# Two projections get the low halves of their weights from ScalarE and an accumulating DMA instead of VectorE

## The chip, the cores and the metric

One core of a Trainium2 chip runs the whole layer, in one launch. The metric is the device time of that launch in microseconds (us); lower is better. Three runs of the kernel before gave 801.69, 801.78 and 803.82 us, so the median is 801.78 us.

The engines that matter here are PE (TensorE, matrix products), ACT (ScalarE), DVE (VectorE), POOL (GpSimd) and SP, which issues most DMAs. Each engine works through its own list of instructions strictly in order. A DMA that an engine issues runs on 16 DMA engines afterwards; the issuing engine waits only until the DMA may start.

## The reference, cut to what matters

The input is 512 tokens of width 1024 in float32. One normalised copy `h` of it is multiplied by one wide weight, and the result is cut into the inputs of two branches (an mLSTM and a sparse attention) and of two gates:

```python
h = rmsnorm(x, norm1_w)
proj = h @ w_in
(mq, mk, mv, mo, mi, mf, nq, kc, vc, ks, vs, kw, vw, ng, gm, gn) = jnp.split(proj, split_pts, axis=-1)
...
kc_t = to_groups(apply_rope(rmsnorm(kv_heads(kc), kcmp_norm_w), cos, sin))
kw_t = to_groups(apply_rope(rmsnorm(kv_heads(kw), kwin_norm_w), cos, sin))
...
x = x + y @ w_out
return x + (a * v) @ ffn_w_down
```

`kw` and `vw` are the third keys and values (of the window attention), `ng` its gates, `mi` and `mf` the mLSTM's gates, `mv` the mLSTM's values.

## The kernel before

All products that are large run as three matmuls over split operands. A float32 weight is split into a high half H (rounded to the type fp32r that PE takes at its fast rate) and a low half L, which is the weight less H. The activations are split the same way, into `hTH` and `hTL`. The product is then the sum of activation-high by H, activation-high by L, and activation-low by H (`mm3`, lines 424 to 427). In the profile these three matmuls have the lines 425, 426 and 427, so line 426 is the first that needs L.

**How a weight comes in.** The class `Weights` (from line 31) handles this for every weight. A chunk of up to 1 MB is loaded by a DMA of SP into one of two `raw` buffers (line 68). A chunk has two halves (in the count of this text: C0 and C1 are the halves of the first chunk of projection C). `ensure` (from line 71) converts half after half into one of four `whl` buffers, which hold H and L side by side. H is always a copy on ACT (line 88). L has three forms, chosen by sets that are filled at lines 291 to 294:

- DVE subtracts (line 94), the form for the halves of the change in the kernel before;
- POOL subtracts (line 94 as well, two halves at the start);
- ACT writes the rounded negative of the weight (line 91), and POOL issues a DMA that adds the raw weight to it (line 92).

`ensure` also issues the load of the next chunk (line 68) once the chunk two before it has been used. That load overwrites the `raw` buffer of that earlier chunk, so SP holds it until whatever reads this buffer last is done: the subtractions of DVE, or the accumulating DMAs.

**The order of the work.** The order on every engine is written out by hand through a table of numbers (`PLAN`, from line 104). Projection B (first keys and values, 512 columns) runs first. The next projections form one stream, `proj_stream` (from line 743): C (288 columns: `kw`, `vw`, `ng`, `mi`, `mf`), A (queries, 512 columns), MV (the mLSTM's values, 512 columns), then gates and others. A `Filler` hands out this stream step by step between the steps of the attention's preparation. `tok_group` (line 456) calls `ensure` for the half three ahead, at a step that the table names. So A0 is converted at the end of C's second quarter; C0 to C2 are converted during the last token tile of B (line 651), and C3 in C's first quarter.

The preparation of attention follows in the program after the conversions of A0. It begins with `rope_norm` (line 658): squares on ACT (line 667), sums on DVE (line 668), then the rope of the first keys on DVE. Behind that rope, still in DVE's order, stand the copies of the gate columns out of the accumulators of C (`evac_c`, line 703, done by line 235). The accumulators of A's first two token tiles lie in the two PSUM buffers that C's first two tiles used, so PE can begin A only when these copies are done. The compression of the keys and values (line 785, `ph`) needs the sums that DVE writes at line 778.

The lines that the change and the steps of the prediction touch are these: 68 (load of raw), 88 and 91 (ACT), 92 (DMA of POOL), 94 (DVE), 235 (copies), 425 to 427 (matmuls of C, A and MV), 667 and 668 (`rope_norm`), 778 and 785 (compression), 683 (part of the rope on POOL), 846 to 849 (transposes of the queries).

Of the kernel before, what the change touches and what calls it, by code (L numbers as in the profile page):

```python
# [97 lines left out]
def bcast(ap, n):  # L98
# [18 lines left out]
    "p_sc21": 0, "p_sc30": 0, "p_sc31": 1, "poolA": 2, "poolC": 0, "poolGM": 2, "poolGN": 2, "poolMO": 2,  # L117
    "poolMQK": 2, "poolMV": 0, "poolUM": 2, "poolUN": 2, "poolWO": 2, "q2_eb": 1, "q2_ex0": 0, "q2_ex1": 0,
# [1520 lines left out]
```

## Time and profile before

| what | value |
|---|---|
| median of three runs | 801.78 us |
| the profiled execution's own time | 804.88 us |
| span of its instructions | 803.0 us |
| share of the span in which PE works on matmuls | 97% |
| DVE, ACT, POOL busy | 57%, 47%, 27% |
| bytes moved by DMA, mean rate | 132.18 MB, 165 GB/s |
| mean granted clock of PE | 0.993 of full speed |

The profiled execution is 3.1 us (0.4%) longer than the median of the plain runs. The span runs from the first instruction to the last one. Start times in the rows below are microseconds from the span's start. Lines of a timeline give the start, the duration, the engine, the line of the kernel, the operation, what it writes and reads, its shape, how many were merged, and in brackets the idle time of this engine just before and what ended it.

### The profile page before, as it was taken

The page shows a single profiled execution, that of the slowest core. Times are in us where ns is not written, and L with a number is a line of the kernel's source. Part 1 is how long each engine was busy: PE and PEld are TensorE (multiplying, and loading weights), DVE is VectorE, ACT ScalarE, POOL GpSimd, SP SyncE. Part 2 cuts the span into 40 slices and gives each one's busy share as a digit, 9 for nine tenths or more (in the row PEclk, how much of TensorE's full clock was granted, in tenths as well). Part 3 has the DMA queues.
Part 4 walks back from the last instruction along what each step waited for, and adds up shares of the span by engine and source line. Part 5 has one row for each costly group of instructions (what it writes and reads, how often), then busy time and mean ns, then how long its engine had stood idle before and what let it go on. Part 6 is the DMA issues. An engine that isn't in the chain of part 4 may idle for free.

```text
span 803.0 us, 10557 instructions
## 1 busy us (share of the span) xinstructions
PE 779.3 (97%) x4037; PEld 643.3 (80%) x4037; DVE 460.2 (57%) x817; ACT 379.5 (47%) x637; POOL 218.9 (27%) x227
## 2 busy tenths in 40 slices
PE   8999989999999999999879999999999999999898
PEld 5797878878788878878668998888888888888786
DVE  4576775686565654544525545554554554554776
ACT  6344546645565595583523343333333333443552
POOL 5320121220111122122200008855554443200600
PEclk9999999999999999999999999999999999999999
DMA  6884168565555567359885338675545444575372
GB/s 229 279 225 141 20 140 131 106 113 98 105 105 106 106 105 131 79 114 184 183 284 190 147 108 293 239 251 210 199 174 194 178 145 158 204 274 177 120 232 107
DMA packets 97059, 132.18 MB, mean 165 GB/s; under 512 B 6607, under 2 KB 75375, under 8 KB 95600
## 3 DMA queue, kind: packets, MB, share of 16 engines
q1 hardware_dynamic: 63054, 91.64, 34.4%
q0 software_dynamic: 33952, 39.85, 24.4%
q8 instruction: 32, 0.52, 0.3%
q14 instruction: 19, 0.16, 0.1%
q10 hardware_dynamic: 2, 0.00, 0.0%
HBM read 94.79 MB, written 15.73 MB: 138 GB/s over the span
## 4 chain that ended last, share of the span: by engine, by line
PE 73%; issue 8%; DMA 7%; DVE 6%; ACT 4%; POOL 2%; POOLq 0%; SPq 0%; DVEq 0%; ACTq 0%
PE ff L1355 10%; PE ff L1354 10%; PE ff L1356 10%; DMA whl<-raw 4%; PE P L426 3%; PE P L427 3%; PE P L425 2%; PE on L946 2%; PE ptp L935 2%; PE gm L487 1%; PE gm L489 1%; PE gm L488 1%; PE sp L905 1%; PE wo L426 1%; PE wo L427 1%
## 5 line engine op out<-in xcount | busy, mean ns | idle before, releaser
L88 ACT ACTIVATE whl<-raw 128x1024 fp32r<-128x1024 f32 (+2 forms) x144 | 144.9, 1011 | 145.0 <-PE ff L1356 57.2
L94 DVE TENSOR_TENSOR whl<-raw,whl 128x1024 fp32r<-128x1024 f32 (+1 forms) x102 | 127.6, 1260 | 146.0 <-ACT whl L88 146.0
L1354 PE MATMUL ff<-h2H,whl 128*128 128x512 f32 (+1 forms) x384 | 142.8, 372 | 0.0
L1355 PE MATMUL ff<-h2L,whl 128*128 128x512 f32 (+1 forms) x384 | 142.6, 371 | 0.0
L1356 PE MATMUL ff<-h2H,whl 128*128 128x512 f32 (+1 forms) x384 | 142.6, 371 | 0.0
L92 POOL DMA_DIRECT2D whl<-raw x40 | 54.8, 1371 | 231.6 <-ACT whl L91 223.0
L1354 PEld LDWEIGHTS ff<-h2H,whl 128*128 128x128 f32 x384 | 72.3, 188 | 12.6
L1356 PEld LDWEIGHTS ff<-h2H,whl 128*128 128x128 f32 x384 | 72.3, 188 | 12.5
L1355 PEld LDWEIGHTS ff<-h2L,whl 128*128 128x128 f32 x384 | 72.3, 188 | 12.3
L920 ACT ACTIVATE P<-sp,nmx 128x128 f32<-128x128 f32 (+3 forms) x64 | 33.1, 524 | 36.7 <-DVE nmx L911 36.5
L91 ACT ACTIVATE whl<-raw 128x1024 fp32r<-128x1024 f32 x40 | 41.9, 1048 | 0.0
L1406 ACT ACTIVATE ct<-ct 128x512 f32<-128x512 f32 x22 | 13.9, 633 | 54.1 <-DVE ct L1404 54.1
L911 DVE TENSOR_REDUCE nmx<-sp 128x2 f32<-128x256 f32 (+3 forms) x32 | 26.2, 818 | 17.9 <-PE sp L908 17.8
L425 PE MATMUL P<-whl,g 128*128 128x512 f32 x88 | 34.2, 389 | 0.0
L426 PE MATMUL P<-whl,g 128*128 128x512 f32 x88 | 34.2, 389 | 0.0
L427 PE MATMUL P<-whl,g 128*128 128x512 f32 x88 | 34.2, 389 | 0.0
L1404 DVE SCALAR_TENSOR_TENSOR ct<-ff,vcol,ct 128x511 f32<-128x511 f32 (+1 forms) x44 | 32.7, 744 | 2.2 <-ACT ct L1402 1.4
L1412 ACT ACTIVATE g<-ct 128x512 fp32r<-128x512 f32 x22 | 13.9, 632 | 37.0 <-DVE ct L1416 21.9
L426 PE MATMUL wo<-whl,yH 128*128 128x512 f32 x64 | 25.6, 400 | 4.1 <-DMA whl<-raw 4.1
L235 DVE COPY P<-ptp 128x256 f32<-128x256 f32 (+1 forms) x32 | 17.7, 554 | 19.3 <-PE ptp L935 19.2
L426 PE MATMUL P<-whl,sb 128*128 128x512 f32 x66 | 25.9, 393 | 2.5 <-DVE whl L94 2.3
L1413 DVE TENSOR_TENSOR g<-ct,g 128x512 fp32r<-128x512 f32 x22 | 15.4, 699 | 21.9 <-ACT g L1412 21.9
(400 smaller groups left out, 1795.0 us busy)
## 6 DMA issues: line engine op xcount, KB each, us to landing
raw<-in_ffn_w_up_dram SPq DMA_DIRECT2D x22, 1024.0 KB, 5.1
whl<-raw POOLq DMA_DIRECT2D x40, 512.0 KB, 5.7
raw<-in_w_in_dram SPq DMA_DIRECT2D x16, 1024.0 KB, 5.0
st<-in_ffn_w_down_dram SPq DMA_DIRECT2D x11, 1024.0 KB, 7.5
td<-st POOLq DMA_DIRECT2D x11, 1024.0 KB, 4.2
raw<-td SPq DMA_DIRECT2D x22, 512.0 KB, 5.4
raw<-in_ffn_w_down_dram SPq DMA_DIRECT2D x11, 512.0 KB, 4.2
raw<-in_w_out_dram SPq DMA_DIRECT2D x4, 1024.0 KB, 8.1
```

Source lines behind the costliest of these rows:

```text
L88: nc.scalar.activation(h, src, AF.Copy)
L91: nc.scalar.activation(l, src, AF.Copy, scale=-1.0)
L92: nc.gpsimd.dma_start(l, src, accum_op=ALU.add)
L94: (nc.gpsimd if n in self.on_pool else nc.vector).tensor_sub(l, src, h)
L425: pe.matmul(o, aH, bH, start=start, stop=False)
L426: pe.matmul(o, aH, bL, start=False, stop=False)
L427: pe.matmul(o, aL, bH, start=False, stop=stop)
L920: act.activation(Pv[:, y], sv[:, y], AF.Exp, bias=nmx[:, y:y + 1], accum_out=den[:, y:y + 1])
L1354: pe.matmul(acc[:, a:b], H[:, k, :], hh, start=(k == 0), stop=False)
L1355: pe.matmul(acc[:, a:b], H[:, k, :], hl, start=False, stop=False)
L1356: pe.matmul(acc[:, a:b], L[:, k, :], hh, start=False, stop=(k == KD - 1))
L1404: dve.scalar_tensor_tensor(t[:, k:], a[:, :S - k], col("ffn_conv_w", (2 - k) * NF + m), t[:, k:], op0=ALU.mult, op1=ALU.add)
```

## The change

Two numbers of the table become 2. With 2, all halves of a projection go into the set `on_dma`, and their low half takes the third of the forms above. With 0, none of them do. The projections are C (`poolC`) and MV (`poolMV`), each with four halves. A half of C has 2 x 288 = 576 columns of float32 in each of 128 partitions (294,912 bytes), a half of MV 2 x 512 = 1024 (524,288 bytes). Nothing else is changed: neither the places at which the halves are converted nor the order of the other work.

```diff
-    "p_sc21": 0, "p_sc30": 0, "p_sc31": 1, "poolA": 2, "poolC": 0, "poolGM": 2, "poolGN": 2, "poolMO": 2,
-    "poolMQK": 2, "poolMV": 0, "poolUM": 2, "poolUN": 2, "poolWO": 2, "q2_eb": 1, "q2_ex0": 0, "q2_ex1": 0,
+    "p_sc21": 0, "p_sc30": 0, "p_sc31": 1, "poolA": 2, "poolC": 2, "poolGM": 2, "poolGN": 2, "poolMO": 2,
+    "poolMQK": 2, "poolMV": 2, "poolUM": 2, "poolUN": 2, "poolWO": 2, "q2_eb": 1, "q2_ex0": 0, "q2_ex1": 0,
```

The lines of `ensure` between which the sets choose are these:

```python
nc.scalar.activation(h, src, AF.Copy)
if n in self.on_dma:

    nc.scalar.activation(l, src, AF.Copy, scale=-1.0)
    nc.gpsimd.dma_start(l, src, accum_op=ALU.add)
else:
    (nc.gpsimd if n in self.on_pool else nc.vector).tensor_sub(l, src, h)
```

## Rows read from the trace of the kernel before

**Rows 1.** Busy time of each engine in three stretches (from and to, length, then PE, PEld, DVE, ACT and POOL with busy us and instructions, PE's granted clock, share and rate of the DMA engines). The first holds projection C and the start of A, the second the rest of A, the third MV.

```profile
30.00:60.00 30.00, 29.82 (x179) 26.47 (x177) 19.24 (x44) 13.20 (x25) 4.26 (x5) 1.00 0.84 242
60.00:94.00 34.00, 33.65 (x204) 27.16 (x203) 23.52 (x52) 16.64 (x30) 1.61 (x4) 1.00 0.30 87
94.00:118.00 24.00, 21.62 (x113) 17.43 (x112) 20.43 (x32) 8.98 (x14) 6.90 (x6) 1.00 0.59 120
```

**Rows 2.** What PE waited for between 30 and 130 us, longest first (total us, times, longest).

```profile
PE pq L846 <- DVE qdup L235: 1.8, 3, 1.1
PE pq L846 <- ACT qdup L233: 0.6, 1, 0.6
```

**Rows 3.** The group of DVE's subtractions for low halves between 30 and 130 us (count, then busy us and mean ns, then idle time before).

```profile
L94 DVE TENSOR_TENSOR whl<-raw,whl 128x576 fp32r<-128x576 f32 (+1 forms) x8 | 7.9, 988 | 6.3 <-ACT whl L88 6.3
```

**Rows 4.** ACT's timeline from the conversion of C0 to the squares of `rope_norm`. The four conversions with 576 columns are C0 to C3; those at 43.76 and 44.72 are H and the negative of A0.

```profile
35.29 0.69 ACT L88 ACTIVATE whl<-raw 128x576 fp32r<-128x576 f32 x1 [3.88 <-issue]
37.11 0.69 ACT L88 ACTIVATE whl<-raw 128x576 fp32r<-128x576 f32 x1 [1.13 <-PE aBs L427]
39.22 0.69 ACT L88 ACTIVATE whl<-raw 128x576 fp32r<-128x576 f32 x1 [1.42 <-DMA raw<-in_w_in_dram]
...
40.07 0.67 ACT L88 ACTIVATE whl<-raw 128x576 fp32r<-128x576 f32 x1
43.76 1.06 ACT L88 ACTIVATE whl<-raw 128x1024 fp32r<-128x1024 f32 x1 [3.01 <-DMA raw<-in_w_in_dram]
44.72 1.04 ACT L91 ACTIVATE whl<-raw 128x1024 fp32r<-128x1024 f32 x1
45.67 0.61 ACT L667 ACTIVATE rqk<-kraw 128x512 f32<-128x512 f32 x1
```

**Rows 5.** SP's timeline, three of its loads of raw chunks: the first chunk of A at 38.62, the first of MV at 55.08, and the second of the gates (GM) at 98.42.

```profile
38.62 0.37 SPq L68 DMA_DIRECT2D raw<-in_w_in_dram  x1
...
55.08 0.37 SPq L68 DMA_DIRECT2D raw<-in_w_in_dram  x1
...
98.42 0.37 SPq L68 DMA_DIRECT2D raw<-in_w_in_dram  x1
```

**Rows 6.** POOL's timeline: its DMAs for A0 and A1, then a part of the first query's rope and the DMA of GM0.

```profile
46.08 1.07 POOL L92 DMA_DIRECT2D whl<-raw  x1 [17.92 <-ACT whl L91]
50.51 0.87 POOL L92 DMA_DIRECT2D whl<-raw  x1 [3.35 <-ACT whl L91]
...
94.50 0.88 POOL L683 TENSOR_TENSOR rtq<-qraw,tab 128x256 f32<-128x256 f32 x1 [26.08 <-DVE qraw L679]
96.05 1.61 POOL L92 DMA_DIRECT2D whl<-raw  x1 [0.67 <-ACT whl L91]
```

**Rows 7.** All accumulating DMAs up to 130 us from issue to landing; a DMA of POOL of 256 KB (count, KB, median us to landing); and the busy times (columns as in the first group) of the two microseconds in which the DMA of A0 moved its 512 KB.

```profile
DMA to landing us min/median/max: 4.4/5.6/6.1
...
out_dram<-x1r POOLq DMA_DIRECT2D x2, 256.0 KB, 2.5
...
48.00:50.00 2.00, 2.00 (x17) 2.00 (x16) 1.43 (x6) 1.97 (x4) 0.00 (x0) 1.00 1.12 217
```

**Rows 8.** DVE's timeline: the subtraction for C1, the sums of `rope_norm`, the copies of the gate columns of C's first two token tiles, the sums for the compression, and the subtraction for MV3 with what follows it.

```profile
37.83 0.76 DVE L94 TENSOR_TENSOR whl<-raw,whl 128x576 fp32r<-128x576 f32 x1 [0.96 <-ACT whl L88]
...
46.32 1.28 DVE L668 TENSOR_REDUCE rss<-rqk 128x8 f32<-128x512 f32 x2 [3.56 <-ACT rqk L667]
...
52.44 0.28 DVE L235 COPY gts<-aC 128x32 f32<-128x32 f32 x2
...
61.63 2.67 DVE L778 TENSOR_TENSOR X<-pz,pet 64x496 f32<-64x496 f32 x4
...
97.18 1.21 DVE L94 TENSOR_TENSOR whl<-raw,whl 128x1024 fp32r<-128x1024 f32 x1
98.70 1.30 DVE L849 TENSOR_TENSOR QS<-pq,QS 64x512 fp32r<-64x512 f32 x2 [0.32 <-ACT QS L848]
```

**Rows 9.** PE's timeline: the first matmul of C that needs a low half, and the first matmul of A; then from the chain of waits the start of the compression (start, length).

```profile
39.70 0.29 PE L426 MATMUL aC<-whl,hTH 128*128 128x288 f32 x1
...
53.12 0.47 PE L425 MATMUL aA<-whl,hTH 128*128 128x512 f32 x1
...
64.55 7.13 PE ph L785 x64
```

**Rows 10.** ACT's timeline, two places: the copies of H of MV3 and GM0 (merged), and that of GM2, the first half of GM's second chunk.

```profile
92.60 2.20 ACT L88 ACTIVATE whl<-raw 128x1024 fp32r<-128x1024 f32 x2
...
117.26 1.04 ACT L88 ACTIVATE whl<-raw 128x1024 fp32r<-128x1024 f32 x1
```

**Rows 11.** Busy times (columns as in the first group) in three pairs of stretches: one in which PE stood idle for most of the time, and one soon after it.

```profile
10.00:12.00 2.00, 0.18 (x2) 0.07 (x1) 0.09 (x1) 1.76 (x4) 2.00 (x2) 1.00 1.05 309
13.00:17.00 4.00, 4.00 (x14) 3.08 (x13) 3.36 (x9) 2.30 (x4) 1.84 (x3) 0.57 0.69 264
...
384.00:387.00 3.00, 0.43 (x2) 0.00 (x0) 0.69 (x2) 2.28 (x3) 0.88 (x1) 1.00 0.55 88
389.00:392.00 3.00, 3.00 (x8) 2.30 (x7) 2.25 (x4) 2.51 (x3) 0.82 (x1) 0.50 1.03 304
...
414.00:418.00 4.00, 0.31 (x2) 0.00 (x0) 0.00 (x0) 0.48 (x1) 0.00 (x0) 1.00 0.72 205
419.50:422.50 3.00, 3.00 (x8) 2.31 (x7) 1.47 (x2) 0.03 (x1) 0.00 (x0) 0.50 0.96 310
```

## The prediction

> **What bounds the kernel now.** I read the busy times by stretch first, then PE's waits, then the timelines of ACT, SP, POOL, DVE and PE around projection C. In the first two stretches PE is busy for 29.82 of 30 us and 33.65 of 34 us [rows 1], so PE sets the pace there and DVE, with 19.24 and 23.52 us, does not. In the third, PE is idle for 2.38 us, and its waits for the queries' rope account for it, 1.8 + 0.6 us [rows 2]. So work taken from DVE can only win in that third stretch, and anything that makes PE late earlier goes straight into the time.
>
> What to see in ACT's timeline is that the supply of weights is tight at one place. ACT stood idle for 3.01 us until the raw chunk of A had landed, converted A0 at 43.76, wrote its negative at 44.72, and only then could start the squares of `rope_norm` at 45.67 [rows 4]. DVE waited 3.56 us for these squares [rows 8]. So the landing of A's first chunk sets the start of a chain on ACT and DVE. SP issued that load at 38.62 [rows 5], right when DVE's subtraction for C1 ended, 37.83 + 0.76 = 38.59 [rows 8]: C0 and C1 lie in the `raw` buffer that the load overwrites.
>
> **The change part by part.** Removed are eight subtractions, 7.9 us of DVE [rows 3]. Added are eight activations on ACT and eight DMAs on POOL.
>
> *C0 and C1, on the path.* Copies of 576 columns that follow each other would start 0.59 us apart (a copy of 1024 columns takes 1.06 us and its successor starts after 0.96 us, so 0.10 us less than the 0.69 us of one [rows 4]). So C1's H starts at 37.11, its negative at 37.70, ending near 38.38. POOL's DMA for A0 started 0.32 us after its negative ended (44.72 + 1.04 = 45.76 to 46.08 [rows 4, 6]); C1's would start at 38.70.
>
> How long until the sum has landed? The nearest row is A1's DMA of 512 KB: issued at 50.51, and SP, which waits for it, goes on at 55.08, so 4.57 us [rows 5, 6]. Such a DMA moves 217 GB/s [rows 7], so 0.524 MB takes 2.42 us, and C's 0.295 MB 1.36 us: I take 4.57 - 1.06 = 3.5 us. The ends of the range are 2.5 us (a POOL DMA of 256 KB without a sum) and 6.1 us (the slowest accumulating one up to 130 us) [rows 7]. So C1 is done at 42.2 and SP issues A's load 3.6 us later than before. C2's and C3's own accumulating DMAs then run beside that load; alone each moves for 1.36 us, and I take 0.5 us of delay from them (ends 0 and 1.4). A's chunk lands 4.1 us late; call this S.
>
> A rule speaks for a smaller S. The Trainium skill, page "DMA: Bandwidth & Descriptors", section "Anatomy of one DMA — SWDGE (gpsimd) path", puts one such DMA at some 2.0 us plus its bytes at 436 GB/s. That is an estimate of 2.68 us for C1 and an S of 3.2 us. For A1's 512 KB it gives 3.20 us where the trace has 4.57 us, so I stay with the row.
>
> ACT is idle before A0 [rows 4], so S shifts A0's conversion, the squares, and DVE's chain behind them in full. In that chain stand the copies of C's gate columns at 52.44 [rows 8]; two merged in 0.28 us, so the first is out by 52.62. A's first matmul started at 53.12 [rows 9] and needs the accumulator that the copy frees: 0.50 us of margin, so PE begins A 4.1 - 0.5 = 3.6 us late.
>
> *The low half of C0, inside that.* By the same steps C0's negative ends at 36.56, its DMA starts at 36.88 and lands at 40.4, or at 41.4 by the full 4.57 us; PE wants it at 39.70 [rows 9]. PE stands for 0.7 to 1.7 us. This does not add to the 3.6 us, because PE would only wait less before A: some 1.9 to 2.9 us.
>
> *PE's clock.* In three places PE stood idle: 1.82 of 2 us from 10, most of 384 to 387, and 3.69 of 4 us from 414. Soon after each the granted clock was 0.57 or 0.50, the lower of its two levels (1.2 GHz) for most or all of the stretch. Eight matmuls took 3.00 us from 389 to 392 and from 419.5 to 422.5 [rows 11]; at the full clock they take half, so each drop costs 1.5 us, and 1.6 us with its edges. The waits before the queries' transposes, none over 1.1 us [rows 2], left the clock at 1.00 [rows 1]. A wait of 1.9 to 2.9 us lies on the side of those that lost the clock. I take a drop as somewhat likelier than none: 3.6 + 1.6 = 5.2 us.
>
> Without a drop another margin sets the sum: DVE's sums for the compression end at 64.30 [rows 8] and the compression started at 64.55 [rows 9], 0.25 us later. They follow S, so PE is 4.1 - 0.25 = 3.85 us late there.
>
> *C2, C3, MV0 to MV3, beside other work.* C2 and C3 give A's second chunk late, but its conversions now stand behind an ACT that is itself late. MV's low halves have long leads. The last, MV3, shows the tightest case: its H starts at 92.60 [rows 10], its negative ends near 94.6, POOL's rope work ends at 95.38 [rows 6], so the DMA lands about 100.0 and GM's second chunk is loaded 1.5 us later than 98.42 [rows 5]. GM2 is converted at 117.26 [rows 10], so more than 10 us of cover remain. POOL issues MV3's DMA before GM0's (96.05), which moves that by some 1 us; the next part of rope on POOL comes one token tile later. Were this cover gone, the cost would be those 1.5 us.
>
> *What DVE wins.* MV3's subtraction ends at 98.39, but DVE then waits 0.32 us for ACT [rows 8], so the loop of the queries does not become shorter. I take nothing.
>
> **Sum.** The profiled execution took 804.88 us, 1.88 us around its span of 803.0, and would take 804.9 + 5.2 = 810.1. It is 3.1 us over the median; the same 5.2 us on the median of 801.78 give 807.0 us. No stage behind makes this up: PE is the bound, and its later waits keep their place relative to it.
>
> **Rivals.**
> - *The clock holds.* For it: a wait of 1.9 us is hardly longer than the shortest that lost the clock, and that one came early, amid light work. Against it: all three long ones lost it. Then 801.78 + 3.85 = 805.6 us.
> - *The short DMA.* If C1's sum lands after 2.5 us, S is 38.70 + 2.5 - 38.62 = 2.6, and PE loses 2.6 - 0.25 = 2.3 us with the clock held: 804.1 us, which cannot be told from no change. Against it: that row has no sum and half the bytes.
> - *The long DMA.* With 6.1 us and the full 1.4 us from C2 and C3, S is 7.6, PE begins A 7.1 us late and loses the clock: 801.78 + 7.1 + 1.6 = 810.5 us. For it: C0's DMA starts while loads still run.
> - *Faster.* DVE, relieved of four subtractions among the queries' ropes, hands over earlier, and PE's idle time of 2.38 + 0.35 us in the last two stretches [rows 1] goes, to 799.0 us. It decides only if A's chunk is no later than before, that is if C1's sum landed by 38.6, before its DMA has even started. And the 0.32 us of DVE behind MV3 speak against the gain.
>
> **How the numbers follow.** Chances: lost clock (forecast) 0.45, held clock 0.27, short DMA 0.12, long DMA 0.12, faster 0.04. Within 0.3%, about what a measurement of this kernel can tell, is 2.4 us: 799.4 to 804.2. So slower has the first two, the long DMA and a little of the short one, 0.85; no change the rest of the short one, 0.11; faster 0.04. The likeliest case alone spans 805.8 to 808.6 us (S from 2.9 to 5.7). The range of 8 in 10 is 803.6 to 809.6 us: it leaves out the faster case, and the upper half of the long DMA.
>
> **What would show it.** In ACT's timeline, A0's H about 4 us later than 43.76 and its idle time before it near 6 us, ended by the raw load; in SP's, the load held by the accumulating DMA until about 42. In PE's waits, one of about 1 us for C's low half and one of 2 to 3 us at A's start for the gate columns' copy, then eight to nine matmuls at the lower clock. If A starts on time, or if PE's waits for the queries' ropes shrink, the prediction is wrong.

## The result, and the profile after

The changed kernel took 807.75 us (median of four runs, 807.38 to 809.48), the kernel before 802.49 us (four runs, 801.69 to 803.82): 5.3 us slower, a ratio of 1.0062 with a 95% interval of 1.0045 to 1.0080. The profiled execution of the changed kernel took 807.84 us (span 806.0), only 3.0 us more than the profiled one of before (804.88, span 803.0). Why the two profiled executions differ by less than the medians is taken up at the end of this section. One run of the kernel before, among those taken beside the experiments, took 1295.26 us at a granted clock of 0.56; the ratios leave it out, and they are not the quotients of the medians beside them.

The busy times by stretch answer to [rows 1], with the same columns:

```profile
30.00:60.00 30.00, 25.64 (x153) 22.97 (x152) 9.87 (x28) 14.66 (x27) 5.55 (x8) 0.94 0.87 232
60.00:94.00 34.00, 33.23 (x202) 26.73 (x201) 20.59 (x48) 15.47 (x25) 5.88 (x8) 1.00 0.64 164
94.00:118.00 24.00, 22.24 (x113) 18.07 (x112) 19.21 (x33) 11.70 (x20) 7.37 (x8) 1.00 0.56 113
```

DVE's busy time fell in each stretch. In the first it fell by 9.4 us, of which C's four subtractions of 0.76 us are 3.0; the rest is work that now comes later. PE lost 4.2 us of work there: it executed 153 matmuls instead of 179. What PE waited for between 30 and 130 us says where (compare [rows 2]):

```profile
PE aC L426 <- DMA whl<-raw: 2.4, 1, 2.4
PE aA L425 <- DVE gts L235: 1.8, 1, 1.8
PE pq L846 <- DVE qdup L235: 1.8, 3, 1.1
PE pq L846 <- ACT qdup L233: 0.6, 1, 0.6
PE ph L785 <- DVE X L778: 0.5, 1, 0.5
```

The waits for the queries' rope are the same 1.8 and 0.6 us as before, so the relief of DVE shortened neither. Three waits are new: for the low half of C0, for the gate columns before A, and a short one before the compression.

The chain behind them is read in four timelines. First POOL's DMAs for C0, C1 and C3, which did not exist before:

```profile
37.18 1.07 POOL L92 DMA_DIRECT2D whl<-raw  x1 [8.34 <-ACT whl L91]
38.98 0.87 POOL L92 DMA_DIRECT2D whl<-raw  x1 [0.73 <-PE aBs L427]
...
44.19 0.86 POOL L92 DMA_DIRECT2D whl<-raw  x1 [0.56 <-ACT whl L91]
```

Then SP's loads of A's first and second chunk (38.62 [rows 5] and 41.92 us before). Each is held until the sums that read its buffer have landed:

```profile
44.13 0.37 SPq L68 DMA_DIRECT2D raw<-in_w_in_dram  x1
51.93 0.37 SPq L68 DMA_DIRECT2D raw<-in_w_in_dram  x1
```

Then ACT: H and negative of C0, the wait for A's chunk, and A0 with the squares of `rope_norm` behind it (compare [rows 4]). The idle 6.78 us before A0 are put down to PE here; in two other profiles with the same wait (6.74 us in a second execution of the changed kernel, 6.80 us with C alone) they are put down to the raw load.

```profile
35.60 0.69 ACT L88 ACTIVATE whl<-raw 128x576 fp32r<-128x576 f32 x1 [3.89 <-issue]
36.19 0.67 ACT L91 ACTIVATE whl<-raw 128x576 fp32r<-128x576 f32 x1
...
50.68 1.06 ACT L88 ACTIVATE whl<-raw 128x1024 fp32r<-128x1024 f32 x1 [6.78 <-PE aCs L427]
51.64 1.04 ACT L91 ACTIVATE whl<-raw 128x1024 fp32r<-128x1024 f32 x1
52.59 0.61 ACT L667 ACTIVATE rqk<-kraw 128x512 f32<-128x512 f32 x1
```

And PE, which came to C's first low half at 42.55 instead of 39.70 us and began A at 59.59 instead of 53.12 us [rows 9]:

```profile
42.55 0.40 PE L426 MATMUL aC<-whl,hTH 128*128 128x288 f32 x1 [2.38 <-DMA whl<-raw]
...
59.59 0.50 PE L425 MATMUL aA<-whl,hTH 128*128 128x512 f32 x1 [1.77 <-DVE gts L235]
```

A0's H is 50.68 - 43.76 = 6.9 us late, A 6.5 us, the compression (71.5 against 64.55 us) 6.9 us. The 0.5 us between the first two is the margin that the prediction read off [rows 8, 9].

**Where 4 us came back.** The lateness stays at 6.9 us until the up-projection of the mLSTM (`um`) begins at 376.7 us, and is 3.1 us when `w_out`'s product (`wo`) begins. The profiled execution of before lost time in between that this one did not: it waited there 3.2 us for DVE and 0.5 us for a sum, and its clock fell to 0.50 in 389 to 392 us [rows 11]. The changed kernel waited 1.9 us and kept the clock:

```profile
387.00:390.00 3.00, 1.21 (x6) 0.67 (x4) 0.69 (x1) 2.41 (x3) 0.11 (x1) 1.00 1.24 197
...
390.00:393.00 3.00, 2.84 (x12) 2.36 (x13) 2.12 (x4) 0.92 (x3) 0.77 (x1) 1.00 1.22 210
392.00:395.00 3.00, 3.00 (x15) 2.48 (x14) 2.15 (x4) 2.62 (x4) 0.00 (x0) 1.00 1.06 222
```

That is 3.7 - 1.9 = 1.8 us of waiting and some 1.5 us of clock. What ends last there is the first load of `w_out`: 8.2 us from SP's issue (375.54) to ACT's conversion (383.76) in the profile of before, 6.3 us (381.25 to 387.59) after. Whether a late front brings the shorter wait, one profile of each kernel cannot tell. For it: all six profiles of the next section that are 2.7 us late or more at `um` waited 1.4 to 1.9 us for a sum there (the one with the extra buffer another 1.3 us for DVE), while MV alone (0.1 us early) and C0 alone (2.1 us late) waited 3.2 us for DVE like the kernel before. Against it: C by POOL's subtraction, 0.2 us late, waited 1.7 us for a sum and 0.6 us for DVE. The profiled execution of before is also a long one, 804.88 - 802.49 = 2.4 us above its median, that of the changed kernel 0.1 us above its own; 2.3 us is what the profiled pair lacks against the medians. So a front is better compared by its own starts, as in the table of the next section.

### The profile page after: what moved, and what is told of

It reads as the page before. It is cut to its first block, busy times and chain, and to the rows that moved or that the text cites. A ratio compares the mean times of both kernels' runs of the same rounds, so it can differ in the third digit from the quotient of the medians.

```text
span 806.0 us, 10584 instructions
## 1 busy us (share of the span) xinstructions
PE 779.6 (97%) x4037; PEld 644.3 (80%) x4037; DVE 452.8 (56%) x809; ACT 385.6 (48%) x645; POOL 226.1 (28%) x235
## 4 chain that ended last, share of the span: by engine, by line
PE 70%; DVE 9%; issue 8%; DMA 6%; ACT 5%; POOL 1%; SPq 0%; POOLq 0%; DVEq 0%; ACTq 0%
PE ff L1354 10%; PE ff L1356 10%; PE ff L1355 10%; DMA whl<-raw 3%; PE P L426 3%; PE P L427 3%; PE P L425 2%; PE on L946 2%; PE ptp L935 2%; PE gm L487 1%; PE gm L489 1%; PE gm L488 1%; PE sp L905 1%; PE wo L426 1%; PE wo L427 1%
## 5 line engine op out<-in xcount | busy, mean ns | idle before, releaser
L94 DVE TENSOR_TENSOR whl<-raw,whl 128x1024 fp32r<-128x1024 f32 x94 | 119.8, 1284 | 139.0 <-ACT whl L88 139.0
L92 POOL DMA_DIRECT2D whl<-raw x48 | 61.6, 1282 | 250.8 <-ACT whl L91 239.0
L91 ACT ACTIVATE whl<-raw 128x1024 fp32r<-128x1024 f32 (+1 forms) x48 | 48.8, 1017 | 0.0
```

The lines of the kernel that those rows point to most:

```text
L91: nc.scalar.activation(l, src, AF.Copy, scale=-1.0)
L92: nc.gpsimd.dma_start(l, src, accum_op=ALU.add)
L94: (nc.gpsimd if n in self.on_pool else nc.vector).tensor_sub(l, src, h)
```

## The experiments

For every kernel with a disputed front the table gives how late some starts are against the profiled execution of before (its starts are in the first line), and the difference of the medians, which rests on other executions. The kernels are the kernel before with the edit shown further down (the edits are cut to the entries that change); all times are us. An offset is in these numbers that no edit made: C0's H, ACT's first step in C, starts 0.3 us late in the changed kernel, 0.5 us early with C1 alone, 1.1 us late with C2 and C3 alone, and within 0.5 us of before in the others.

| kernel | H of A0 (ACT) | A (PE) | compression (PE) | `um` (PE) | profiled span | medians |
|---|---|---|---|---|---|---|
| before, absolute | 43.76 | 53.12 | 64.55 | 369.8 | 803.0 | |
| changed | 6.9 | 6.5 | 6.9 | 6.9 | 3.0 | 5.3 |
| changed, second execution | 5.3 | 4.9 | 5.3 | 5.2 | 2.3 | 6.3 |
| C alone | 6.8 | 6.4 | 6.9 | 6.8 | 7.1 | 8.4 |
| MV alone | -0.1 | 0.0 | 0.0 | -0.1 | -0.4 | 1.6 |
| C1 alone | 3.5 | 3.0 | 5.6 | 5.6 | 1.6 | 5.4 |
| C0 alone | 2.2 | 1.8 | 2.2 | 2.1 | 3.2 | 4.4 |
| C2 and C3 alone | 1.0 | 1.1 | 2.8 | 2.7 | -1.5 | 3.1 |
| C on DMA, A's load in a buffer of its own | 5.6 | 6.4 | 6.3 | 6.3 | 5.3 | 8.0 |
| C by POOL's subtraction | 0.1 | -0.3 | 0.1 | 0.2 | -1.0 | -0.5 |

The medians follow the lateness at `um` to within 2.3 us; the profiled span misses it by up to 4.2 us (2.7 against -1.5).

### Which of the two projections: C alone, MV alone

```diff
-"poolC": 0        # C alone: one number
+"poolC": 2
-"poolMV": 0       # MV alone: the other
+"poolMV": 2
```

> Only C's four halves take the accumulating DMA; MV stays with DVE. Theory (the cost sits in C: the late low half of C0 and the raw buffer that C1's sum holds): as slow as the changed kernel, 4.5 to 7 us over the kernel before, PE waits of about 2.4 us for C's low half and 1.8 us before A. Rival (MV's part costs too, through ACT or POOL ahead of the queries' ropes): 2 us or more faster than the changed kernel.

> Only MV's four halves take the accumulating DMA; C stays with DVE. Theory: the same as the kernel before within 1 us, A's first matmul at 53 us, PE's waits for the queries' ropes unchanged at about 2.4 us in sum. Rival (DVE's relief helps the queries' ropes): up to 2.4 us faster with these waits shorter. Other rival (MV costs): 2 us or more slower.

C alone: 809.93 against 801.56 us, a ratio of 1.0102 (1.0079 to 1.0125). MV alone: 803.11 us, 1.0015 (1.0000 to 1.0030), with its front on time and the waits for the queries' rope at 1.7 us. Its median is 1.6 us above that of before, between the theory's 1 us and the 2 us of the rival that MV costs. So the cost is C's. C alone repeats the front of the changed kernel almost to the tenth (waits of 2.8 us in C and 1.8 us before A). But its 8.4 us are more than the 4.5 to 7 us expected, and 2 to 3 us more than the changed kernel lost; the intervals of the ratios just meet. The two profiles begin `um` within 0.1 us of each other, and their spans differ by 4.1 us. Two later waits are the same in both, 1.9 us in `um` and 2.3 us in the last product (`P`), but with C alone the clock fell behind each of them:

```profile
390.50:393.50 3.00, 3.00 (x8) 2.27 (x9) 2.27 (x4) 1.22 (x2) 0.35 (x1) 0.55 1.21 211
...
763.18 0.79 PE L426 MATMUL P<-whl,sb 128*128 128x512 f32 x1 [2.32 <-DVE whl L94]
764.00:766.00 2.00, 2.00 (x6) 1.52 (x6) 2.00 (x4) 0.00 (x0) 0.26 (x1) 0.50 0.00 0
```

`wo` begins 1.8 us later than in the changed kernel, and `P` loses another 1.4 us. The kernel before has the same wait in `P`, and kept the clock behind it:

```profile
757.99 0.50 PE L426 MATMUL P<-whl,sb 128*128 128x512 f32 x1 [2.33 <-DVE whl L94]
758.50:760.50 2.00, 2.00 (x10) 1.63 (x10) 2.00 (x4) 0.00 (x0) 0.59 (x1) 1.00 0.00 0
```

So most of the 4.1 us is clock. Whether the same sets the medians apart was not followed up.

### The changed kernel once more

```diff
-"poolC": 0, "poolMV": 0
+"poolC": 2, "poolMV": 2
```

> The changed kernel once more, for a second trace and more times. Theory: up to the first matmul of the up-projection of the mLSTM branch (um) it is again 6 to 7 us behind the kernel before; from there to the down-projection its distance is anything from 3 to 7 us, because the wait for the first chunk of w_out there differs from one execution to the next in both kernels. Rival (the change itself shortens the wait in um): the distance falls to 3 us again.

808.39 against 802.07 us, 1.0070 (1.0045 to 1.0094). At `um` it is 5.2 us late, less than the 6 to 7 us expected, and over the span 2.3 us, which is what the rival said, though the medians lie 6.3 us apart. Its front is cleaner than that of the first execution: SP issued the first of three loads of chunks at 29.98 instead of 31.48 us (31.39 with C alone), and C2 could be converted at 39.66 instead of 41.22 us, so the first sums met less of these loads (that this made the difference is not shown). PE's waits, and the clock in two stretches, during and behind the wait before A:

```profile
PE aA L425 <- DVE gts L235: 3.2, 1, 3.2
PE aC L426 <- DMA whl<-raw: 1.3, 1, 1.3
```

```profile
54.70:57.90 3.20, 0.05 (x1) 0.00 (x0) 3.03 (x8) 3.20 (x7) 1.02 (x2) 1.00 1.06 220
58.50:62.00 3.50, 3.50 (x17) 2.86 (x17) 3.29 (x8) 0.00 (x0) 0.83 (x2) 1.00 1.05 206
```

The wait in C is 1.1 us shorter and the one before A 1.4 us longer than in the first execution; and a wait of 3.2 us left the clock at 1.00. C1's sum ran from 38.52 to 42.57 us, when SP went on, so 4.05 us; A's load took 42.57 to 49.07, 6.5 us instead of the 43.76 - 38.62 = 5.14 us of before. ACT's line for A0:

```profile
49.07 1.06 ACT L88 ACTIVATE whl<-raw 128x1024 fp32r<-128x1024 f32 x1 [6.74 <-DMA raw<-in_w_in_dram]
```

So S, the lateness of that chunk, is 5.3 us, and the compression is late by the same 5.3 us.

### C1 alone: the raw buffer

```diff
+    W.on_dma |= set([T_C[1]])
     for i in T_WO[4:]:
```

> Only C1 takes the accumulating DMA, so PE's first need of a low half of C is met by DVE as before. Theory (two separate costs): no PE wait at C's first low half and at most 1 us at its second quarter, but A's raw chunk is loaded 4 to 5.5 us later than 38.6, the squares start that much later and PE begins A 3 to 5 us late; 3 to 6 us over the kernel before. Rival (the stall at C0 and the clock that it costs are the whole price, the held raw buffer is hidden): within 1 us of the kernel before.

806.98 against 801.56 us, 1.0067 (1.0044 to 1.0090). Here PE finds C0's low half in time, and there is one wait alone:

```profile
PE aA L426 <- DVE gts L235: 3.3, 1, 3.3
```

POOL issued the sum at 38.17 and SP the load at 42.20: 4.03 us. The load took 5.0 us, as before, since no other sum ran beside it. So A0's H is late by 3.5 us, A by 3.0 us. Then the clock fell, as two windows show (during and behind the wait), and the compression came 5.6 us late:

```profile
52.90:56.10 3.20, 0.00 (x0) 0.00 (x0) 3.03 (x9) 3.20 (x8) 1.01 (x2) 0.83 0.45 88
56.50:60.00 3.50, 3.50 (x9) 2.73 (x9) 3.36 (x7) 0.00 (x0) 0.84 (x1) 0.50 1.05 205
```

Nine matmuls in 3.5 us, where the second execution of the changed kernel has 17 behind a wait as long. This is the predicted course, sum, load, chain, wait, clock, by itself, within the 3 to 6 us expected.

### C0 alone: the late low half

```diff
+    W.on_dma |= set([T_C[0]])
```

> Only C0 takes the accumulating DMA. Theory: PE waits 2 to 2.5 us at C's first low half and runs some 14 matmuls at the lower clock, and A's raw chunk is held by C0's sum until about 42.4, 3.8 us later than before, so that PE begins A 3.5 to 5 us late, of which 4 are already lost in C; 3.5 to 5.5 us over the kernel before. Rival (the held raw buffer is the whole price): A begins 3.3 us late at most, and the stall in C only takes the place of the wait before A.

805.94 against 801.56 us, 1.0047 (1.0030 to 1.0064). PE's waits in the front:

```profile
PE aC L427 <- DMA whl<-raw: 1.4, 1, 1.4
PE ph L786 <- POOL vbd L815: 0.5, 1, 0.5
```

C0's sum was issued at 36.62 us and SP went on at 41.05, 4.43 us later. It holds the raw buffer as well, though it starts before C1's would. A0's H is 2.2 us late and so is the compression: 1.4 us of it are lost in C, 0.5 us right before the compression, with the clock held. The expected wait of 2 to 2.5 us with slow matmuls and the A that is 3.5 to 5 us late did not come: A is 1.8 us late without a wait of its own, which is what the rival allowed, so this run does not show the stall apart from the hold. C1 alone is later at the compression (5.6 against 2.2 us), in part by the clock; the medians (5.4 and 4.4 us) do not separate the two.

### C2 and C3 alone

```diff
+    W.on_dma |= set(T_C[2:])
```

> Only C2 and C3 take the accumulating DMA. Theory: no PE wait in C, the load of A's first chunk is issued at 38.6 as before and lands at most 2 us later beside the two sums; A begins less than 1.5 us late. Rival (what costs is the sums' traffic beside A's load, not who holds the buffer): A's first half is converted 3 us late or more and A begins 3 us late.

805.18 against 802.07 us, 1.0034 (1.0011 to 1.0056). This execution is about 1.1 us late from the start on, and A begins late by no more than that. The sums were issued at 41.81 and 43.21 us, over 2 us behind the load of A's first chunk (39.72 us), and it took 5.0 us, none the longer. Yet the compression lost another 1.7 us. The prediction had named the way and set it aside: "C2 and C3 give A's second chunk late, but its conversions now stand behind an ACT that is itself late". Here ACT is on time, and waits for that chunk:

```profile
PE ph L786 <- POOL vbd L815: 1.8, 1, 1.8
```

```profile
56.05 1.06 ACT L88 ACTIVATE whl<-raw 128x1024 fp32r<-128x1024 f32 x1 [3.58 <-DMA raw<-in_w_in_dram]
57.96 0.26 ACT L233 ACTIVATE kraw<-aCs 128x128 f32<-128x128 f32 x1
...
58.25 0.29 DVE L235 COPY vst<-aCs 128x128 f32<-128x128 f32 x1 [1.84 <-ACT kraw L233]
59.43 1.28 POOL L687 TENSOR_TENSOR rtk<-kraw,tab 128x512 f32<-128x512 f32 x1 [0.24 <-DVE kraw L680]
64.47 2.66 DVE L779 TENSOR_TENSOR X<-pz,pet 64x496 f32<-64x496 f32 x4
```

A's second chunk could be loaded at 47.63 instead of 41.92 us, and its first half was converted at 56.05 instead of 51.26 us. Behind this in ACT's order stands the copy of `kraw`, which DVE waits for, and behind DVE the rope on POOL (56.58 us before). DVE's last sums for the compression end at 67.13 instead of 64.30 us, and PE follows 0.26 us later, as before. The profile names POOL's `vbd`, which ended at 67.19 us; but what line 786 reads is `X`. In the changed kernel the chain of A's first chunk is later than this and hides it.

### A buffer of its own for A's load

```diff
-"poolC": 0
+"poolC": 2
+    W.rawdst[W.halves[T_A[0]][0]] = opage
```

> C's four halves take the accumulating DMA, but the first raw chunk of A is loaded into a free page, so that no sum holds its load. Theory (two costs, the stall at C0 with the lost clock and the held raw buffer): the stall at C's first low half and the slow matmuls stay, C ends 4.4 us late, but A begins without a wait of its own, 4.4 us late instead of 6.5. Rival (the lateness of A comes from ACT or from C's buffers, not from the held load): A is still 6 us late or more.

810.03 against 802.07 us, 1.0085 (1.0053 to 1.0116): no gain. With another page of memory to go to, A's load was issued at 34.97 us and did not wait. PE's waits between 30 and 75 us begin with:

```profile
PE aC L427 <- DMA whl<-raw: 4.7, 1, 4.7
```

The wait before A is gone, but C0's sum, issued at 36.74, now shared the DMA engines with that load of 1 MB, and PE got its low half at 44.44 us, 7.7 us later. A is 6.4 us late as before, where 4.4 us was expected; A0's H (49.37 us) now waits for PE and not for the load. What the load wins, the sum loses.

### C by POOL's own subtraction

```diff
+    W.on_pool |= set(T_C)
```

> C's four halves leave DVE, but for a subtraction on POOL instead of ACT's negative and a DMA. Theory (the DMA's lateness is the cost, not where the work goes): no PE wait in C and none before A, A's load issued at most 1.5 us later than 38.6; within 1.5 us of the kernel before. Rival (C suffers from any move away from DVE): 3 us or more slower.

802.17 against 802.70 us, 0.9986 (0.9967 to 1.0005). DVE is relieved of C's subtractions as by the change, without a DMA. POOL takes 1.43 us for a half, and SP's load of A goes out on time:

```profile
38.86 0.37 SPq L68 DMA_DIRECT2D raw<-in_w_in_dram  x1
```

PE waits neither in C nor before A. So it is the transfer that costs, not the move away from DVE; and DVE's relief in C by itself buys nothing that can be measured.

### A version that beats both: `um` and `w_out`

In the stage of `um`, the product with `w_up_m`, the kernel before already uses the accumulating DMA, and PE waits there. Other forms were tried for it: its halves back on DVE, then on POOL; `w_out`'s first four halves on POOL; both on POOL.

```diff
-"poolUM": 2                          # on DVE: this line alone
+"poolUM": 0
+    W.on_pool |= set(F_UM)           # on POOL: with this line
-"poolWO": 2
+"poolWO": 0
+    W.on_pool |= set(T_WO[:4])       # w_out on POOL
```

> The kernel before, with the low halves of the mLSTM's up-projection (UM, four halves of 1024 columns) taken from the accumulating DMA and given to DVE. Theory (a sum that holds a raw buffer makes the next load late): the first chunk of w_out is loaded some 5 us earlier, PE's wait of 3.2 us in um and the lower clock behind it go, 3 to 5 us faster than the kernel before. Rival (DVE's four subtractions delay the products that follow um, or the wait only moves to the next chunk of w_out): within 1 us of the kernel before or slower.

> The kernel before with UM's four low halves subtracted by POOL, so that no sum holds w_out's first load and DVE keeps its order free. Theory: w_out's first chunk is loaded 8 us or more earlier, PE's waits in um go and no new one in un appears, 3 to 5 us faster than the kernel before. Rival (the wait moves on to w_out's next chunks, whose low halves are still sums): within 1.5 us.

> The kernel before with the low halves of w_out's first four pieces subtracted by POOL; UM keeps its sums. Theory: PE's wait of 4.1 us for a low half in the down-projection and the slow matmuls behind it go, 4 to 6 us faster; the wait in um stays. Rival (the x loads, which POOL issues behind, become late): the wait stays or moves to the transposes of the second norm.

> Both of these together. Theory: the two gains add, 7 to 10 us faster than the kernel before, with no PE wait for a low half left between un and the feed-forward part. Rival (one load behind them bounds both): no more than the better one alone.

On DVE: 801.65 against 802.07 us, 1.0001 (0.9978 to 1.0023). The wait in `um` goes, and one for DVE's gate of the other branch takes its place, already in `un`, the product before; the time is the rival's:

```profile
PE un L507 <- DVE gn L741: 3.7, 3, 2.5
```

On POOL, whose subtractions take 2.5 us for a half of 1024 columns: 799.32 against 802.70 us, 0.9966 (0.9949 to 0.9982), faster than both kernels and within the 3 to 5 us expected (3.4 us in the medians). `w_out`'s first load goes out at 364.95 instead of 375.54 us, since no sum holds its buffer, and PE waits in `um` for nothing more; the wait in `wo` stays. SP's load, then all of PE's waits from 346 to 450 us:

```profile
364.95 0.37 SPq L68 DMA_DIRECT2D raw<-in_w_out_dram  x1
```

```profile
PE wo L427 <- DMA whl<-raw: 4.5, 1, 4.5
PE un L508 <- DVE gn L742: 1.0, 1, 1.0
```

`w_out` on POOL: 801.56 us, 0.9987 (0.9971 to 1.0003), not the 4 to 6 us expected. Both: 799.84 us, 0.9966 (0.9947 to 0.9984). The gains do not add, as the rival said: without the sums, PE waits for DVE's gate in both stages. PE's waits with both on POOL:

```profile
PE um L508 <- DVE gm L1291: 2.6, 2, 1.6
PE wo L426 <- DVE gm L1291: 2.3, 1, 2.3
```

## Why the prediction was right, and where its sum was not

**Direction and size.** 807.0 us was predicted, 807.75 us measured; +5.2 us against +5.3 and, in the second comparison, +6.3. Of the two steps said to cost time, C1's sum holding A's load is shown alone; C0 late for PE is shown by its own wait, but in a run in which C0's sum holds A's load too. DVE's relief wins nothing, as predicted, and MV costs little or nothing (its interval reaches from 0 to 0.3%).

**The chain from A's load to PE held.** "S shifts A0's conversion, the squares, and DVE's chain behind them in full", with 0.50 us of margin before A and 0.25 us before the compression. With S read from A0's H, 6.9, 5.3, 6.8, 3.5 and 2.2 us in five profiles, A is late by S less 0.4 to 0.5 us in each (with C0 alone without a wait before A). The compression is late by S itself in the four whose clock held behind A. The margin of 0.25 us was misread: it is the time from DVE's last sums to PE's start also when PE waits for them (71.22 to 71.48 us in the changed kernel).

**S was mis-sized: 4.1 us predicted, 5.3 and 6.9 us measured.** Two terms of it failed.
- "I take 4.57 - 1.06 = 3.5 us" for C1's sum. It took 4.03 us alone, and behind C0's 4.05 us in the second execution, 44.13 - 38.98 = 5.15 us in the first and 5.57 us with C alone. (That SP went on 3.6 us late with C1 alone, as predicted, is luck: the front began 0.5 us early there.) The step scaled the row of A1's sum by bytes at the rate of a busy window. On the lowest readings, 0.524 to 0.295 MB saved only 4.57 - 4.03 = 0.54 us, an estimate of 425 GB/s for what grows and of 3.3 us for what does not. C0's and C3's sums, each in a run beside a load, took 4.43 and 4.42 us at C's size, so the rate is rough. The Trainium skill, page "DMA: Bandwidth & Descriptors", section "Anatomy of one DMA — SWDGE (gpsimd) path", has 436 GB/s for the part that grows and a fixed 2.0 us: the lowest readings agree with the first and show more than the second. (By that rule S comes to 3.3 us, where the prediction has 3.2.)
- "I take 0.5 us of delay" from the sums of C2 and C3. A's load took 6.5 us in both executions of the changed kernel, against 5.14 us before and 5.0 us with C1 alone: 1.4 to 1.5 us, the upper end. With C2 and C3 alone their sums started over 2 us behind the load and cost it nothing; who is first seems to count.

**C0's wait** was put at 0.7 to 1.7 us and measured 2.4, 1.3, 1.4 (alone) and 2.8 us (C alone). As predicted it does not add to the rest: 1.1 us more in C is 1.4 us less before A.

**The clock was a term too many.** "I take a drop as somewhat likelier than none", 1.6 us behind the wait before A. A row of the kernel before speaks against it that the prediction did not read: the wait of 2.33 us in `P`, shown with C alone, kept the clock, so "all three long ones lost it" left out one of just the length in question. In the first execution the clock fell already behind C0's wait:

```profile
44.00:47.00 3.00, 3.00 (x14) 3.00 (x14) 0.26 (x2) 0.00 (x0) 0.86 (x1) 0.50 0.98 188
47.00:49.00 2.00, 2.00 (x16) 2.00 (x16) 0.00 (x0) 0.00 (x0) 0.00 (x0) 0.96 0.98 275
```

There it cost nothing, since the slower matmuls of C only shortened the wait before A (1.8 us). In the second execution it did not fall at all. So the sum came out right by errors against each other, and that the number is this close is luck. The prediction added 1.6 - 0.5 = 1.1 us to S, clock less margin, where nothing was to be added; and its S was too small by 1.2 to 2.8 us. C1 alone is the one run in which the clock was paid behind A: from 3.0 us at A the lateness grew to 5.6 us at the compression. Of the rivals, the held clock was right on the clock behind A in both executions, and its 805.6 us was too low by S; the long DMA with its S of 7.6 us told the first execution's S better than the forecast did; its time failed by the clock too.

**"Its later waits keep their place"** failed for the profiled pair. From the start of `um` to that of `wo` the profiles took 23.6 to 27.8 us, in kernels with and without the change, and it is why the profiled spans differ by 3.0 us only.

**What stays open.** Why C alone is slower than the whole change in the medians (8.4 against 5.3 and 6.3 us), what lets the clock fall behind a wait in one execution and not in another, whether MV's 1.6 us is real, and whether the late front shortens the wait in `um` or the profiles differ there by chance; the two profiles of the changed kernel agree there to 0.2 us.

## What to carry to other kernels

A low half that comes through an accumulating DMA takes a subtraction off DVE, but keeps its consumer waiting and its source buffer held for 4 to 8 us, where the subtraction took about 1 us: ask first which load waits for that buffer, and what waits for that load. A spare engine that does the same subtraction in place (POOL, 1.43 to 2.5 us here) gives the relief and holds the buffer no longer than the subtraction; moving `um` to it saved 0.34%. Compare a front by the starts of its own landmarks, since a stage 300 us behind may have a different wait in each profile.

## What the runs showed of the hardware

Accumulating DMAs hold the DMA engines busy and move less than loads. Two windows of the changed kernel, the first before C's sums, the second with those of C0 and C1 under way:

```profile
34.00:36.00 2.00, 2.00 (x10) 1.42 (x9) 0.19 (x1) 0.40 (x1) 0.00 (x0) 1.00 1.09 384
40.00:42.00 2.00, 0.17 (x2) 0.00 (x0) 0.00 (x0) 0.78 (x2) 0.00 (x0) 1.00 0.93 174
```

The rate falls from 384 to 174 GB/s at nearly the same busy share; with A0's sum in the kernel before it was 217 GB/s at 1.12 [rows 7]. A sum of C's size beside a load of 1 MB came 7.7 us after its issue: C3's, issued at 44.19, let SP go on at 51.93 us (as late in the second execution and with C alone), and C0's in the kernel with the extra buffer took as long. Where the load had a start of over 2 us (C2 and C3 alone), C3's sum took 4.42 us.

The clock is not decided by the length of a wait alone: 3.3 us before A lost it (C1 alone), 3.2 us at the same place kept it (second execution); 1.9 us in `um` kept it (changed kernel) and lost it (C alone); 2.3 us in `P` kept it (before) and lost it (C alone); 2.4 us in C lost it.
